# Four blocks of w_out instead of two in the slots of the projections' weights

## The chip, the cores and the metric

The kernel runs on one core of a Trainium2 chip. Its time is the device time of one execution in microseconds; before the change the median of three runs is 1167.86 us (1167.72 to 1168.35). Besides, one execution was recorded by the hardware profiler: it took 1168.21 us, of which 1166.4 lie between its first and its last instruction (the span). All rows below are from that execution.

The engines of a core work in parallel, each in its own order: TensorE (PE; its weight loads are listed as PEld) multiplies matrices into PSUM banks, VectorE (DVE) and ScalarE (ACT) work element by element, SyncE (SP) issues the transfers between HBM and the on-chip memory (SBUF), one after the other.

## The reference

The reference is one block of a hybrid transformer on x of 1024 positions by 1024 channels, in float32. An input projection `u = x @ w_in` feeds three branches: a gated causal convolution (256 channels), a chunked mLSTM (256 channels) and a differential attention with four heads (512 channels). Then:

```
h = concatenate([y_conv, y_ml, y_da]) @ w_out        # 1024 x 1024
x = layer_norm(ALPHA * x + h, ln1_g, ln1_b)
h = square(relu(x @ w_up)) @ w_down                  # 4096 hidden channels
x = layer_norm(ALPHA * x + h, ln2_g, ln2_b)
```

The change concerns the product with `w_out` and the residual `ALPHA * x`.

## The kernel before

**Precision.** Every float32 operand of a large product is split in two: ScalarE rounds it (`act.copy`, line 147, written `hi`, `th`, `yh`), VectorE subtracts the rounded value from the original (line 148, written `lo`, `tl`, `yl`). A product is the sum of three matmuls: hi x hi, lo x hi, hi x lo. A block of weights (128 x 1024) thus takes three slots while it is split, raw, hi and lo, and two after.

**Slots.** The SBUF buffers are 47 slots of 128 x 1056 words (`Slots`, line 54). Each ring is a queue of slot numbers: `alloc` takes the first, `free` appends at the end, so the order of allocations in the program decides which older buffer a new one lies in, and the new one's first writer waits for the last reader of the old. Ring X (slots 0 to 15) holds x, split; ring W (nine slots, 16 to 24) the weights of the input projections; ring T two slots for the projections' results; ring G the rest.

**Order.** A scheduler places the instructions of each engine when the program is built; a `lane` gives their priority: 1 (loads, splits, evacuations) goes before 2 (the mLSTM and the attention), 3 (the projections) and 6 (the output projection). The order is fixed in the program then, and each engine follows it and waits where it must.

**The place.** TensorE interleaves the attention of heads 0 to 2 with the input projections. The last of them (`proj_last`, line 193) goes through x in eight steps and frees two slots of X after each. Its two results lie in the two PSUM banks of `ps_mm` until ScalarE has written `th` and VectorE `tl`, half by half; these go to HBM (`qk<-th`, `qk<-tl`).

Behind it comes the output projection in two parts. Part one (`row1`, line 914) takes the first five blocks of `w_out`: 128 positions at a time (row 0 to row 7), two banks of 15 matmuls each, 240 in all; VectorE then adds ALPHA times the residual row, which was loaded from x (`acc<-in_x`, line 894). For each row five pieces of the branches' outputs are loaded (`yraw`) and split (`yh`, `yl`). Part one fills TensorE while the attention's heads 2 and 3 wait for ScalarE and VectorE. In the attention, `s` are scores, `pp` their exponentials, `t` the transposed ones, `wth` and `wtl` their halves, and `t<-wth,vh` and its like the product with the values. Part two (`row2`) takes blocks 5 to 7 (`wo2`), which lie in slots that part one frees, during the attention of head 3. Then follow the two large products with `w_up` and `w_down`.

The lines around the change:

```
839    early = [load_split(W, a["w_out"][kb], D) for kb in range(NEARLY)]
871                xa = (W if tb < NW - 2 * NEARLY else X).alloc(F32, "acc")
872                load(xa[:, :D], a["x"][tb])
917            early += [load_split(X, a["w_out"][kb], D) for kb in range(NEARLY, 5)]
918        row1(tb, [t for t in ((0, 1) if tb == 0 else (tb + 1,)) if t < TB])
919    for r, w in zip([W] * NEARLY + [X] * (5 - NEARLY), early):
920        r.free(*w)
921    X.give(W.take(2 * NEARLY))
```

With NEARLY = 2 blocks 0 and 1 go to W (their slots are those of earlier projections), blocks 2, 3 and 4 to slots that x leaves. Rows 0 to 4 of the residual (tb < 9 - 4) go to W, rows 5 to 7 to X.

Of the kernel before, what the change touches and what calls it, by code (L numbers as in the profile page):

```python
# [26 lines left out]
NSLOT = 47  # L27
NW = 9
NT = 2
NEARLY = 2  # L30
TCARGS = dict(schedule_with_timeline_sim=False)
EPS = 1e-5
ALPHA = 2.0 ** 0.25
# [64 lines left out]
def mixer_block(ctx: ExitStack, tc: tile.TileContext, a: dict, out: bass.AP):  # L98
# [18 lines left out]
    def load(out, in_):  # L117
        nc.sync.dma_start(out=out, in_=in_)
# [43 lines left out]
    def load_split(ring, src, n, ahead=True):  # L162
        with lane(1) if ahead else nullcontext():
            raw = ring.alloc(F32, "raw")
            load(raw[:, :n], src)
            h, l = ring.alloc(F32R, "hi"), ring.alloc(F32R, "lo")
            split(raw[:, :n], h[:, :n], l[:, :n])
            ring.free(raw)
        return h, l
# [483 lines left out]
    def proj_head(h):  # L653

        for j in range(2):
            th, tl = T.alloc(F32R, "th"), T.alloc(F32R, "tl")

            def take(half, cs, ps):
                if j == 0:
                    act.activation(th[:, cs], ps, AF.Copy, scale=0.125)  # L660
                    dve.scalar_tensor_tensor(out=tl[:, cs], in0=ps, scalar=0.125,
                                             in1=th[:, cs].bitcast(F32), op0=ALU.mult,
                                             op1=ALU.subtract)
                else:
                    split(ps, th[:, cs], tl[:, cs])

            (proj_last if 2 * h + j == 7 else proj_fm)(8 + 2 * h + j, take)
            with lane(1):
                move(qkdram[h][2 * j], th[:, :S])
                move(qkdram[h][2 * j + 1], tl[:, :S])  # L670
            T.free(th, tl)
# [166 lines left out]
    proj_head(3)  # L838
    early = [load_split(W, a["w_out"][kb], D) for kb in range(NEARLY)]
    qk_of, v_of = {}, {}  # L840
# [12 lines left out]
    def out_proj(kbs, first, wo, yring):  # L853
# [10 lines left out]
        def get_y(tb, ln, fetched=None):  # L864
            with ln(1):
# [4 lines left out]
                if first:  # L870
                    xa = (W if tb < NW - 2 * NEARLY else X).alloc(F32, "acc")
                    load(xa[:, :D], a["x"][tb])
# [42 lines left out]
    for tb in range(TB):  # L915
        if tb == 0:
            early += [load_split(X, a["w_out"][kb], D) for kb in range(NEARLY, 5)]
        row1(tb, [t for t in ((0, 1) if tb == 0 else (tb + 1,)) if t < TB])
    for r, w in zip([W] * NEARLY + [X] * (5 - NEARLY), early):
        r.free(*w)  # L920
    X.give(W.take(2 * NEARLY))
    X.give(G.take(6))
# [626 lines left out]
```

## Time and profile before

| | |
|---|---|
| median of three runs | 1167.86 us (1167.72 to 1168.35) |
| profiled execution, its span | 1168.21 us, 1166.4 us |
| TensorE busy | 1136.2 us, 97% of the span |
| VectorE, ScalarE busy | 830.8 us (71%), 577.5 us (50%) |
| TensorE's share of the chain that ended last | 85% |

TensorE is busy nearly all the time, and the chain of work that ended last runs mostly through it. So the time is TensorE's work, plus the stretches in which it waits, plus those in which its clock is granted at the lower of its two levels (1.2 instead of 2.4 GHz). A matmul's row shows its start and its length; the next one starts before its end, since they are pipelined, so the distance of starts is what one costs. In square brackets behind an instruction stands how long its engine was idle before it, and what ended that.

### The profile page before, as it was taken

Reading aid. Unit: us, or ns where it says so; the run is one execution under the profiler, and the core shown is the slowest. Engines: PE = TensorE matmul, PEld = TensorE weight load, DVE = VectorE, ACT = ScalarE, POOL = GpSimd, SP = SyncE. Lnnn points to the kernel's source line nnn. Section 1 sums busy time; section 2 is a strip of 40 time slices with the busy share of each in tenths; the row PEclk is TensorE's granted clock in tenths of the full one; section 3 lists DMA queues with packets and bytes.
Section 4 is the critical chain, followed back from the end, with each engine's and each line's share of the span. In section 5 each row is a group of like instructions: output and inputs, shape, how many; then the busy total and the mean of one; then the engine's idle time right before and its main releaser. Section 6 shows DMA issues by size and latency. Waiting matters only on the chain.

```text
span 1166.4 us, 14925 instructions
## 1 busy us (share of the span) xinstructions
PE 1136.2 (97%) x5630; PEld 930.8 (80%) x5630; DVE 830.8 (71%) x1243; ACT 577.5 (50%) x934; POOL 0.2 (0%) x4
## 2 busy tenths in 40 slices
PE   8999999999999999899999999999999999999996
PEld 6898778877897787677788888888888878888884
DVE  5999658875756547778986767655589677666686
ACT  6212383475665526596654444544545323334461
POOL 0000000000000000000000000000000000000000
PEclk9999999999999999999999999999999999999998
DMA  7202135444635663350466464534894644344321
GB/s 281 73 10 73 37 91 168 154 140 123 196 107 172 213 183 103 111 177 37 153 237 250 165 239 168 204 126 162 307 352 162 198 163 160 111 151 125 104 109 72
DMA packets 81640, 179.86 MB, mean 154 GB/s; under 512 B 7648, under 2 KB 29216, under 8 KB 81568
## 3 DMA queue, kind: packets, MB, share of 16 engines
q1 hardware_dynamic: 81568, 178.91, 45.1%
q8 instruction: 44, 0.72, 0.3%
q14 instruction: 28, 0.23, 0.1%
HBM read 120.12 MB, written 58.72 MB: 153 GB/s over the span
## 4 chain that ended last, share of the span: by engine, by line
PE 85%; DVE 7%; DMA 3%; ACT 3%; issue 2%; SPq 0%; DVEq 0%; ACTq 0%
PE f L944 32%; PE mm L112 26%; PE mm L944 17%; PE s L112 5%; PE t L112 3%; PE t L115 2%; DVE lo L148 1%; DMA kh<-qk 1%; ACT pp L738 1%; DVE acc L967 1%; DMA xraw<-in_xT 0%; DMA vh<-v 0%; DMA hraw<-h 0%; DVE nm L736 0%; DVE pp L744 0%
## 5 line engine op out<-in xcount | busy, mean ns | idle before, releaser
L944 PE MATMUL f<-hi 128*128 128x512 f32 x512 | 201.7, 394 | 1.4 <-DVE acc L1242 1.1
L944 PE MATMUL f<-lo,hi 128*128 128x512 f32 x512 | 201.5, 394 | 0.6 <-DVE lo L148 0.5
L944 PE MATMUL f<-hi,lo 128*128 128x512 f32 x512 | 201.5, 394 | 0.0
L944 PE MATMUL mm<-lo,hi 128*128 128x512 f32 x320 | 125.9, 394 | 0.3 <-DVE lo L148 0.3
L944 PE MATMUL mm<-hi 128*128 128x512 f32 x320 | 126.2, 394 | 0.0
L944 PE MATMUL mm<-hi,lo 128*128 128x512 f32 x320 | 126.1, 394 | 0.0
L944 PEld LDWEIGHTS f<-hi 128*128 128x128 f32 x512 | 96.5, 188 | 24.1 <-DVE acc L1242 1.5
L944 PEld LDWEIGHTS f<-lo,hi 128*128 128x128 f32 x512 | 96.3, 188 | 23.3 <-DVE lo L148 1.5
L944 PEld LDWEIGHTS f<-hi,lo 128*128 128x128 f32 x512 | 96.1, 188 | 22.1
L112 PE MATMUL mm<-xh,hi 128*128 128x512 f32 x240 | 95.8, 400 | 5.1 <-ACT xh L147 5.1
L147 ACT CAST hi<-hraw 128x1024 fp32r<-128x1024 f32 x56 | 58.2, 1048 | 84.9 <-DMA hraw<-h 83.4
L148 DVE TENSOR_TENSOR lo<-hraw,hi 128x1024 fp32r<-128x1024 f32 x56 | 68.2, 1223 | 44.6 <-ACT hi L147 42.4
L112 PE MATMUL mm<-xl,hi 128*128 128x512 f32 x240 | 96.1, 400 | 0.1
L112 PE MATMUL mm<-xh,lo 128*128 128x512 f32 x240 | 96.0, 400 | 0.0
L285 DVE SCALAR_TENSOR_TENSOR cacc<-ypad,pc,cacc 128x1024 f32<-128x1024 f32 x60 | 74.2, 1285 | 0.6
L112 PE MATMUL mm<-hi,xh 128*128 128x256 f32 (+1 forms) x256 | 74.1, 289 | 0.0
L112 PE MATMUL mm<-hi,xl 128*128 128x256 f32 (+1 forms) x256 | 73.2, 286 | 0.0
L112 PE MATMUL mm<-lo,xh 128*128 128x256 f32 (+1 forms) x256 | 73.1, 286 | 0.0
L944 PEld LDWEIGHTS mm<-lo,hi 128*128 128x128 f32 x320 | 60.2, 188 | 14.4 <-DVE lo L148 0.7
L944 PEld LDWEIGHTS mm<-hi 128*128 128x128 f32 x320 | 60.3, 188 | 13.8 <-DVE acc L967 0.3
L944 PEld LDWEIGHTS mm<-hi,lo 128*128 128x128 f32 x320 | 60.1, 188 | 13.8
L147 ACT CAST hi<-B 128x1024 fp32r<-128x1024 f32 x36 | 37.6, 1049 | 52.9 <-PE mm L944 23.9
(278 smaller groups left out, 2309.7 us busy)
## 6 DMA issues: line engine op xcount, KB each, us to landing
hraw<-h SPq DMA_DIRECT2D x56, 512.0 KB, 3.4
w<-in_w_up SPq DMA_DIRECT2D x32, 512.0 KB, 4.5
B<-in_w_down SPq DMA_DIRECT2D x32, 512.0 KB, 4.8
h<-hp SPq DMA_DIRECT2D x16, 512.0 KB
h<-hx SPq DMA_DIRECT2D x16, 512.0 KB, 3.1
h<-hq SPq DMA_DIRECT2D x16, 512.0 KB, 3.3
raw<-in_wfm SPq DMA_DIRECT2D x14, 512.0 KB, 3.5
qk<-th SPq DMA_DIRECT2D x8, 512.0 KB
```

The costliest lines, as they stand in the source:

```text
L112: return nc.tensor.matmul(out, lhsT=lhsT, rhs=rhs, start=start, stop=stop)
L115: nc.tensor.transpose(out, in_, ident[:k, :k])
L147: act.copy(hi, src)
L148: dve.tensor_tensor(out=lo, in0=src, in1=hi.bitcast(F32), op=ALU.subtract)
L285: dve.scalar_tensor_tensor(out=av, in0=yp[:, i:i + S], scalar=col(PC_DWW + 31 * c + i), in1=av, op0=ALU.mult, op1=ALU.add)
L738: act.activation(pp[m][:, 0:nk], s_[:, 0:nk], AF.Exp, bias=nm[:, m:m + 1], accum_out=sm[:, m:m + 1])
L944: return nc.tensor.matmul(out, lhsT=lhsT, rhs=rhs, start=start and not more, stop=stop and not more, skip_group_check=more)
L967: dve.tensor_tensor(out=out, in0=p, in1=q, op=ALU.add)
```

## The change

```diff
-NEARLY = 2
+NEARLY = 4
```

With NEARLY = 4 the same lines do this. Blocks 0 to 3 of `w_out` go to W, block 4 alone to X. Of the residual rows only row 0 lies in W (tb < 9 - 8), rows 1 to 7 in X. Following the queue of W: block 2 gets the slots 16, 17 and 18 for raw, hi and lo, which are raw, hi and lo of the last projection's own weights; block 3's raw goes to block 0's raw slot, its hi to block 1's, its lo to block 2's; row 0 of the residual goes to block 3's raw slot. After part one W hands eight slots to X instead of four. The number of slots in use, of transfers, splits and matmuls is the same.

The scheduler's order changes with it. On VectorE, between the end of the last projection and row 0 of part one, before (`lo_4076`, `lo_4082`, `lo_4088`: blocks 2, 3, 4; `tl_2762`: the last projection's two halves; `yl_4098`: row 0; `wtl_...`: attention; `acc_4101`: sum of row 0):

```order
L148 TENSOR_TENSOR lo_4076<-raw_4073,hi_4075 128x1024
L148 TENSOR_TENSOR lo_4082<-raw_4079,hi_4081 128x1024
L148 TENSOR_TENSOR lo_4088<-raw_4085,hi_4087 128x1024
L148 TENSOR_TENSOR tl_2762<-mm_2769,th_2761 128x512
L148 TENSOR_TENSOR tl_2762<-mm_2770,th_2761 128x512
L148 TENSOR_TENSOR yl_4098<-yraw_4091,yh_4097 128x640
L148 TENSOR_TENSOR wtl_3819<-t_3845,wth_3817 128x4x128
L148 TENSOR_TENSOR wtl_3820<-t_3852,wth_3818 128x128
L894 SCALAR_TENSOR_TENSOR acc_4101<-acc_4101,mm_4116 128x512
L148 TENSOR_TENSOR wtl_3819<-t_3880,wth_3817 128x4x128
L148 TENSOR_TENSOR yl_4110<-yraw_4103,yh_4109 128x640
L148 TENSOR_TENSOR wtl_3820<-t_3887,wth_3818 128x2x128
```

and now (`lo_4088`: block 4; `lo_2840`, `lo_2846`: blocks 2 and 3):

```order
L148 TENSOR_TENSOR lo_4088<-raw_4085,hi_4087 128x1024
L148 TENSOR_TENSOR yl_4098<-yraw_4091,yh_4097 128x640
L148 TENSOR_TENSOR tl_2762<-mm_2769,th_2761 128x512
L148 TENSOR_TENSOR lo_2840<-raw_2837,hi_2839 128x1024
L148 TENSOR_TENSOR tl_2762<-mm_2770,th_2761 128x512
L148 TENSOR_TENSOR lo_2846<-raw_2843,hi_2845 128x1024
L148 TENSOR_TENSOR yl_4110<-yraw_4103,yh_4109 128x640
L148 TENSOR_TENSOR wtl_3831<-t_3857,wth_3829 128x4x128
L148 TENSOR_TENSOR wtl_3832<-t_3864,wth_3830 128x128
L148 TENSOR_TENSOR wtl_3831<-t_3892,wth_3829 128x4x128
L894 SCALAR_TENSOR_TENSOR acc_4101<-acc_4101,mm_4116 128x512
L894 SCALAR_TENSOR_TENSOR acc_4101<-acc_4101,mm_4133 128x512
```

The two `tl` stood behind all three blocks; now the first stands behind block 4 and row 0's `yl`, the second behind block 2. Row 1's `yl` has moved up, and both sums of row 0 now stand together, ahead of the last `wtl`.

On TensorE, a little later, at the first score product after the attention's next product with the values, before (`t_3892`: product with the values; `mm_4133`: row 0, second bank; `s_3988`: scores):

```order
L112 MATMUL t_3892<-wth_3818,vh_3620 128x256
L112 MATMUL t_3892<-wtl_3820,vh_3620 128x256
L112 MATMUL t_3892<-wth_3818,vl_3621 128x256
L112 MATMUL t_3892<-wth_3818,vh_3620 128x128
L112 MATMUL t_3892<-wtl_3820,vh_3620 128x128
L112 MATMUL t_3892<-wth_3818,vl_3621 128x128
L112 MATMUL mm_4133<-hi_4075,yl_4098 128x512
L112 MATMUL s_3988<-kh_3526,q_3523 128x512
L112 MATMUL s_3988<-kl_3529,q_3523 128x512
```

and now (`t_3904`, `s_4000` the same two; `mm_4163`: row 1, first bank):

```order
L112 MATMUL t_3904<-wth_3830,vh_3632 128x256
L112 MATMUL mm_4163<-hi_2827,yh_4109 128x512
L112 MATMUL t_3904<-wtl_3832,vh_3632 128x256
L112 MATMUL t_3904<-wth_3830,vl_3633 128x256
L112 MATMUL t_3904<-wth_3830,vh_3632 128x128
L112 MATMUL t_3904<-wtl_3832,vh_3632 128x128
L112 MATMUL t_3904<-wth_3830,vl_3633 128x128
L112 MATMUL s_4000<-kh_3538,q_3535 128x512
L112 MATMUL s_4000<-kl_3541,q_3535 128x512
```

Ahead of the scores 24 matmuls of part one stood, now 31; the one that stood directly ahead of them is gone, and one of row 1 is put in between the products.

On TensorE, at the first score product of head 3 that reads the second half of its keys, before (`mm_4351`: row 5, first bank; `s_4529`: these scores):

```order
L112 MATMUL mm_4351<-hi_4075,yh_4297 128x512
L112 MATMUL mm_4351<-lo_4076,yh_4297 128x512
L112 MATMUL mm_4351<-hi_4075,yl_4298 128x512
L112 MATMUL mm_4351<-hi_4081,yh_4297 128x512
L112 MATMUL s_4529<-kh_3937,q_3934 128x128
L112 MATMUL s_4547<-kh_3928,q_3925 128x256
```

and now (`mm_4368`: row 5, second bank):

```order
L112 MATMUL mm_4351<-hi_4087,yl_4298 128x512
L112 MATMUL mm_4368<-hi_2827,yh_4297 128x512
L112 MATMUL mm_4368<-lo_2828,yh_4297 128x512
L112 MATMUL mm_4368<-hi_2827,yl_4298 128x512
L112 MATMUL mm_4368<-hi_2833,yh_4297 128x512
L112 MATMUL s_4529<-kh_3949,q_3946 128x128
L112 MATMUL s_4547<-kh_3940,q_3937 128x256
```

Ten matmuls of row 5 stood ahead of the scores, now nineteen.

## Rows read from the trace of the kernel before

**Rows 1.** Stretches: per engine busy us (instructions), granted clock, DMA share, GB/s.

```profile
388.00:391.40 3.40, 3.39 (x8) 2.72 (x9) 1.88 (x3) 0.72 (x2) 0.00 (x0) 0.52 1.00 330
...
510.00:540.00 30.00, 28.43 (x146) 23.14 (x144) 22.67 (x52) 25.70 (x40) 0.00 (x0) 1.00 0.29 110
540.00:570.00 30.00, 28.83 (x122) 22.15 (x123) 29.96 (x33) 20.19 (x25) 0.00 (x0) 1.00 0.10 36
600.00:630.00 30.00, 30.00 (x131) 24.31 (x130) 22.57 (x27) 14.67 (x19) 0.00 (x0) 1.00 0.55 196
```

**Rows 2.** TensorE waits, 385 to 550 us: us in total, times, longest.

```profile
PE mm L112 <- DVE tl L148: 2.5, 1, 2.5
PE mm L112 <- DVE lo L148: 1.7, 2, 1.4
PE mm L112 <- DVE yl L148: 1.6, 1, 1.6
PE s L112 <- DMA kh<-qk: 1.0, 1, 1.0
```

**Rows 3.** Timeline of TensorE, end of the last projection: start, length, instruction.

```profile
384.43 0.39 PE L112 MATMUL mm<-xh,lo 128*128 128x512 f32 x1
...
385.13 0.40 PE L112 MATMUL mm<-xh,lo 128*128 128x512 f32 x1
388.01 0.77 PE L112 MATMUL mm<-hi,yh 128*128 128x512 f32 x1 [2.48 <-DVE tl L148]
```

**Rows 4.** Timeline of ScalarE, the same place.

```profile
382.47 1.05 ACT L147 CAST hi<-raw 128x1024 fp32r<-128x1024 f32 x1 [4.76 <-DMA raw<-in_w_out]
...
385.91 1.07 ACT L147 CAST th<-mm 128x512 fp32r<-128x512 f32 x2
386.86 0.74 ACT L147 CAST yh<-yraw 128x640 fp32r<-128x640 f32 x1
```

**Rows 5.** Timeline of VectorE, the same place.

```profile
383.55 3.71 DVE L148 TENSOR_TENSOR lo<-raw,hi 128x1024 fp32r<-128x1024 f32 x3 [5.32 <-ACT hi L147]
387.18 1.28 DVE L148 TENSOR_TENSOR tl<-mm,th 128x512 fp32r<-128x512 f32 x2
```

**Rows 6.** Timeline of SyncE's DMA issues, the same place.

```profile
377.24 3.05 SPq L118 DMA_DIRECT2D raw<-in_w_out  x3
381.14 4.30 SPq L118 DMA_DIRECT2D yraw<-ydram  x8
...
388.48 0.32 SPq L121 DMA_DIRECT2D qk<-tl  x1
```

**Rows 7.** DMA issues, 386 to 392 us: count, KB each, us to landing.

```profile
qk<-tl SPq DMA_DIRECT2D x1, 512.0 KB, 2.8
```

**Rows 8.** Timeline of ScalarE near 397 us.

```profile
397.25 1.01 ACT L738 ACTIVATE pp<-s,nm 128x896 f32<-128x896 f32 x1 [1.83 <-PE t L112]
```

**Rows 9.** Timeline of TensorE near 397 us.

```profile
395.58 0.31 PE L112 MATMUL t<-wth,vh 128*128 128x256 f32 x1
...
397.57 0.27 PE L112 MATMUL t<-wth,vl 128*128 128x128 f32 x1
...
398.40 0.50 PE L112 MATMUL s<-kh,q 128*128 128x512 f32 x1 [0.27 <-ACT pp L738]
```

**Rows 10.** Timeline of TensorE near 439 us.

```profile
439.09 0.49 PE L112 MATMUL s<-kh,q 128*128 128x128 f32 x2 [1.05 <-DMA kh<-qk]
```

**Rows 11.** Timeline of SyncE's DMA issues near 430 us.

```profile
428.84 1.80 SPq L118 DMA_DIRECT2D acc<-in_x  x2
430.68 1.09 SPq L121 DMA_DIRECT2D kh<-qk  x2
```

**Rows 12.** Timeline of TensorE near 470 us.

```profile
468.84 0.83 PE L115 MATMUL t<-cst,pp 128*128 128x128 f32 x6
...
470.90 0.34 PE L112 MATMUL t<-wth,vh 128*128 128x256 f32 x1
```

**Rows 13.** Timeline of SyncE's DMA issues near 476 us.

```profile
476.00 0.33 SPq L118 DMA_DIRECT2D raw<-in_w_out  x1
```

## The prediction

> **What bounds the kernel now.** I read the table of stretches first [rows 1]. From 600 us on TensorE works 30.00 of every 30 us, and so it goes on to the end: what is gained or lost before 550 us is carried to the last instruction. The reader should then look at the slice 388.0 to 391.4: 8 matmuls and a granted clock of 0.52, mostly the lower of the two levels. The list of TensorE's waits between 385 and 550 us [rows 2] has one entry above all others, 2.5 us behind a VectorE subtraction for `tl`. In TensorE's own timeline [rows 3] it is seen in place: the last projection's last matmul starts at 385.13 and ends at 385.53, the first of row 0 of the output projection starts at 388.01. Before the gap matmuls stand (385.13 - 384.43) / 3 = 0.23 us apart, in the slow slice 3.40 / 8 = 0.43. So this place costs 2.48 us of idleness and 8 x (0.43 - 0.23) = 1.6 us of slow clock.
>
> Why it waits: row 0 needs a PSUM bank that the last projection's result holds until it is cast (`th`) and its rest subtracted (`tl`). ScalarE casts three blocks of w_out from 382.47, and `th` only at 385.91 [rows 4]; VectorE spends 3.71 us from 383.55 on the three blocks' low halves, and `tl` starts at 387.18 [rows 5]. The three blocks are this late because their buffers are slots of x, which the last projection frees as it runs: SyncE issues the loads at 377.24 [rows 6].
>
> **The change part by part.** It adds and removes no instruction; five blocks are loaded and split in either kernel, eight residual rows loaded. It moves blocks 2 and 3 from x's slots to W's, and residual rows 1 to 4 the other way. What was to land in W must still wait for W: block 2's halves go into the slots of the last projection's own weights, so its cast cannot start before that projection's last matmuls; block 3's low half goes into block 2's raw slot. Only block 3's high half and block 4 are ready ahead. So the work between the projections is not removed, but VectorE's order changes: `tl` of the first half now stands ahead of the low halves of blocks 2 and 3.
>
> Term A, the gap. The first half's last matmul starts at 384.43 and lasts 0.39 [rows 3]: 384.82. A `th` cast is 1.07 / 2 = 0.54 [rows 4], a `tl` 1.28 / 2 = 0.64 [rows 5], and in the trace TensorE starts 0.19 after the first `tl` ends (387.18 + 0.64 = 387.82 to 388.01). A hand-over from ScalarE to VectorE takes little (a cast over at 382.47 + 1.05 = 383.52, the subtraction at 383.55); with 0.1 for each of the two that is 386.4, so the gap is 0.9 and 1.6 us are saved. Both casts ahead of `th` must be over: block 4's load is the only one issued at 377.24, landing in at most 382.47 - 377.24 = 5.2 us, cast in 1.05 to 383.5; five loads of `yraw` follow at 4.30 / 8 = 0.54 each [rows 6], so the last leaves at 380.3; with the 2.8 us of a larger transfer [rows 7] it lands at 383.1 and `yh` (0.74 [rows 4]) ends at 384.3, just early enough; with 5.2 us it lands at 385.5 and 1.4 of the 1.6 are lost. Bounds 0.2 to 1.8; I take 1.6, since the queue is empty there but for these loads. What is late next: block 2's low half. Its cast follows `th` at 385.4 and ends at 386.5, its subtraction (3.71 / 3 = 1.24) at 387.8; TensorE has 7 matmuls ahead of it in its order and comes to it at 386.4 + 7 x 0.23 = 388.0. The second bank is wanted after 10 matmuls (388.7) and free at 387.8 + 0.64 = 388.4. Block 3's low half ends at 388.4 + 1.24 = 389.7 and is wanted after 14 (389.7). None of the three stops TensorE by more than 0.1.
>
> Term B, the clock. The idle stretches behind `lo` (1.4) and `yl` (1.6) [rows 2] left the clock at 1.00 (510 to 540 us, [rows 1]), so one of 0.9 should too: 1.6 us saved, bounds 0 and 1.6. The Trainium skill (TensorE: Matmul & The Clock Gate, Part 1: The HAM clock gate) calls the number of slow matmuls "run-variable", because the monitor runs free of the kernel; by that rule no gap is sure to leave the clock alone, and the sum would lack this term. The trace has one slow stretch, behind its longest gap, and none behind the shorter ones, so I keep the term and make the rule a rival.
>
> Term C, the residual of row 0. Its slot is now block 3's raw one, so its load can be issued only at 389.7, behind `qk<-tl` at 388.48 [rows 6]. In VectorE's order the sum of row 0 stands ahead of a `wtl` subtraction that TensorE wants for the attention's second product, after 31 matmuls of the output projection, 6 transposes (0.83 at most [rows 12]) and 13 products of 128 or 256 columns, (397.57 - 395.58) / 17 = 0.12 each [rows 9]: 386.4 + 7.2 + 0.8 + 1.5 = 395.9. I take two sums and the `wtl` like a `tl`, 0.64 each, 1.9 together. A landing 2.8 us after issue [rows 7] is in time (392.5 + 1.9 = 394.4). At 5.2 it is not (396.8, a wait of 0.9). Then comes the next score product: it waits for an exponential of 1.01 us that starts as the second product ends [rows 8, 9]. Before, one matmul covered part of that (0.27 idle); now none does, 0.3 more. Bounds -1.2 and 0; I take -0.4, near the short landing, the nearest row in time and queue.
>
> Term D, the wait for `kh`. In the trace TensorE stands 1.05 us at 439.09 behind a transfer [rows 10] whose issue at 430.68 follows two residual rows at 428.84 [rows 11], released by TensorE itself. That release comes about 2.8 us earlier (A, B, C), and in the new order nine more matmuls of the output projection (9 x 0.23 = 2.1 us) stand ahead of the same score product. TensorE gets there some 0.7 us earlier than now, the transfer 2.8: the wait goes, 1.05 saved, bounds 0 and 1.05.
>
> Term E, where the first part of the output projection runs out. Now six of its matmuls cover the transposed scores' split: transposes at 468.84, product at 470.90 [rows 12]. In the new order one is left there: of 2.06 us some 0.8 stay filled, a new wait of 1.2. In exchange block 7's load, at 476.00 [rows 13] because its slot is freed by the very last of those matmuls, comes that much earlier against the work that wants it, and the 1.4 us behind `lo` [rows 2] shrink to perhaps 0.4. Sum -0.2, bounds -1.2 and +1.7.
>
> After 550 us nothing moves but the names of buffers. VectorE is busy 29.96 of 30 us from 540 to 570 [rows 1]; its work there follows the same rows, so I let it shift with them.
>
> Sum: 1.6 + 1.6 - 0.4 + 1.05 - 0.2 = 3.65 us. From the profiled execution, 1168.21 us (span 1166.4), that gives 1164.6; the median of three runs, 1167.86, lies 0.35 lower, so I predict 1164.2 us.
>
> **The rivals.**
> R1, the clock still falls. Without B the gain is 2.05: 1165.8 us. For it: the one fall came at this very place. Against it: the stretches of 1.4 and 1.6 us without one.
> R2, spent early and waited for later. A and B come, but the attention's own chain keeps its pace; C costs 1.0 of its 1.2, D is not gained, E costs its 1.2: 3.2 - 2.2 = 1.0, 1166.9 us. For it: in the new order the filling matmuls stand further forward at every place I compared (7, then 9, then 5 of them), and VectorE is full from 540. Against it: the named waits apart, no entry in the list of 385 to 550 exceeds 1.0 us [rows 2], so most places have slack.
> R3, slower: the residual row, now late. The transfer for `kh` took from its last issue at 431.2 to 439.05, 7.8 us [rows 10, 11]. If row 0's load does so, it lands at 397.5, the `wtl` is done at 399.4, TensorE stands 3.5 us and the clock falls again, 1.6. Against the 3.2 of A and B, with nothing from D and E, that is 1.9 lost: 1169.8 us. It decides from a landing about 4 us after issue; each further microsecond costs one, and beyond some 2.5 us of idleness the slow clock comes on top. Against it: few transfers are in flight at 390 us.
> That the change does nothing because block 2 must wait anyway is not a case of its own: VectorE's order settles it.
>
> **How the numbers follow.** The forecast 0.52 (its own range 1162.6 to 1165.6), R1 0.11, R2 0.26, R3 0.11. A measurement of this kernel tells about 0.2%, 2.3 us, from no change, so faster means below 1165.5: nearly all of the forecast and a part of R1, and a little of R2, 0.56. Within 0.2%: the rest of R1 and most of R2, 0.33. Slower: R3, 0.11. The range 1162.0 to 1168.4 leaves out some 0.08 below (E at its best) and 0.11 above.
>
> **What would show it.** A: TensorE's gap at the end of the last projection about 0.9 us, first `tl` ahead of two `lo`. B: no stretch near 0.5 of the clock after it. C: the sum of row 0 on VectorE behind a transfer, and no wait of TensorE over 1 us near 396. D: no `kh` in the list of waits. E: a wait behind `wtl` near 467, a shorter one behind `lo`. A sum of TensorE's waits between 385 and 550 that is not about 2 us smaller would make the prediction wrong, and so would a gap of 2 us or more at its old place.

## The result, and the profile after

The changed kernel takes 1162.06 us (median of five, 1161.27 to 1163.77), 0.9947 of the kernel before (95% interval 0.9937 to 0.9958): 5.8 us faster, where 3.65 were predicted. Measured twice more on other chips it is 0.9943 [0.9931, 0.9954] and 0.9957 [0.9944, 0.9969]. The profiled execution took 1163.77 us, span 1162.0.

The stretches after, with the columns of [rows 1]:

```profile
388.00:391.40 3.40, 3.40 (x15) 2.74 (x16) 3.23 (x4) 1.30 (x4) 0.00 (x0) 1.00 0.69 272
472.40:476.00 3.60, 3.52 (x19) 3.52 (x19) 3.60 (x7) 2.85 (x5) 0.00 (x0) 0.59 0.53 165
510.00:540.00 30.00, 29.99 (x161) 24.84 (x160) 24.63 (x52) 25.78 (x39) 0.00 (x0) 1.00 0.22 89
```

Right behind the last projection 15 matmuls run at the full clock, where 8 ran at 0.52. But a stretch with a clock of 0.59 now stands at 472.4. From 510 to 540 TensorE is busy 29.99 us instead of 28.43.

TensorE's waits between 385 and 550 us, to be held against [rows 2]:

```profile
PE t L112 <- DVE wtl L148: 1.9, 1, 1.9
PE s L112 <- DMA kh<-qk: 1.0, 1, 1.0
PE mm L112 <- DVE tl L148: 0.7, 1, 0.7
PE f L944 <- DVE lo L148: 0.5, 1, 0.5
PE t L112 <- ACT sqs L147: 0.3, 1, 0.3
PE mm L112 <- DVE acc L897: 0.3, 1, 0.3
PE s L112 <- ACT pp L738: 0.3, 1, 0.3
PE mm L112 <- DVE lo L148: 0.3, 1, 0.3
```

`tl` 2.5 is 0.7, `lo` 1.7 is 0.3, `yl` 1.6 is gone; `kh` stays; `wtl` 1.9 is new. (`sqs` are the rounded squares for a head's norm, the `acc` of line 897 is a sum of part two; further below, `sm` are the sums of the softmax and `mvf` the statistics of the layer norm.) The projection's end in TensorE's timeline, beside [rows 3]:

```profile
386.88 0.40 PE L112 MATMUL mm<-xh,lo 128*128 128x512 f32 x1
387.98 0.50 PE L112 MATMUL mm<-hi,yh 128*128 128x512 f32 x1 [0.70 <-DVE tl L148]
```

On ScalarE, beside [rows 4], `th` follows the last matmul of its half at once, with only one block (382.72) and row 0's `yh` in front:

```profile
382.72 1.05 ACT L147 CAST hi<-raw 128x1024 fp32r<-128x1024 f32 x1 [3.26 <-DMA raw<-in_w_out]
385.12 0.73 ACT L147 CAST yh<-yraw 128x640 fp32r<-128x640 f32 x1 [1.34 <-DMA yraw<-ydram]
386.61 0.59 ACT L147 CAST th<-mm 128x512 fp32r<-128x512 f32 x1 [0.77 <-PE mm L112]
```

On VectorE, beside [rows 5], `tl` follows it:

```profile
385.88 0.83 DVE L148 TENSOR_TENSOR yl<-yraw,yh 128x640 fp32r<-128x640 f32 x1 [0.85 <-DMA yraw<-ydram]
387.23 0.69 DVE L148 TENSOR_TENSOR tl<-mm,th 128x512 fp32r<-128x512 f32 x1 [0.53 <-ACT th L147]
388.17 1.23 DVE L148 TENSOR_TENSOR lo<-raw,hi 128x1024 fp32r<-128x1024 f32 x1 [0.25 <-ACT hi L147]
```

SyncE, beside [rows 6], issues one block, not three, ahead of the rows of y, and row 0's residual at 391.16:

```profile
378.99 0.33 SPq L118 DMA_DIRECT2D raw<-in_w_out  x1
379.66 5.46 SPq L118 DMA_DIRECT2D yraw<-ydram  x10
...
391.16 0.33 SPq L118 DMA_DIRECT2D acc<-in_x  x1
```

The new wait near 472 us: TensorE's last matmul of part one at 470.11, the product at 472.48.

```profile
469.54 0.82 PE L115 MATMUL t<-cst,pp 128*128 128x128 f32 x6
470.11 0.47 PE L112 MATMUL mm<-hi,yl 128*128 128x512 f32 x1
472.48 0.38 PE L112 MATMUL t<-wth,vh 128*128 128x256 f32 x1 [1.89 <-DVE wtl L148]
```

On VectorE `wtl` could start when its first cast is over, near 470.6 (ScalarE runs the two from 470.18 for 0.86 us); block 6's low half and row 7's sum stand ahead of it:

```profile
470.01 1.22 DVE L148 TENSOR_TENSOR lo<-raw,hi 128x1024 fp32r<-128x1024 f32 x1
471.14 0.68 DVE L894 SCALAR_TENSOR_TENSOR acc<-acc,mm 128x512 f32<-128x512 f32 x1
471.74 0.69 DVE L148 TENSOR_TENSOR wtl<-t,wth 128x512 fp32r<-128x512 f32 x1
```

Blocks 6 and 7 are loaded earlier than before (462.30 and, [rows 13], 476.00):

```profile
455.85 0.33 SPq L118 DMA_DIRECT2D raw<-in_w_out  x1
```
```profile
471.60 0.38 SPq L118 DMA_DIRECT2D raw<-in_w_out  x1
```

### The profile page after: what moved, and what is told of

Read it like the earlier page. It is cut to its first block, busy times and chain, and to the rows that moved or that the text cites. A ratio compares the mean times of both kernels' runs of the same rounds, so it can differ in the third digit from the quotient of the medians.

```text
span 1162.0 us, 14933 instructions
## 1 busy us (share of the span) xinstructions
PE 1135.4 (98%) x5630; PEld 931.4 (80%) x5630; DVE 832.1 (72%) x1243; ACT 578.5 (50%) x934; POOL 0.2 (0%) x4
## 4 chain that ended last, share of the span: by engine, by line
PE 86%; DVE 7%; DMA 3%; ACT 2%; issue 1%; SPq 0%; DVEq 0%; ACTq 0%
PE f L944 32%; PE mm L112 26%; PE mm L944 17%; PE s L112 5%; PE t L112 4%; PE t L115 2%; DVE lo L148 1%; DMA kh<-qk 1%; DMA xraw<-in_xT 1%; DVE nm L736 1%; DVE acc L967 1%; ACT pp L738 0%; ACT hi L147 0%; DMA vh<-v 0%; DVE pp L744 0%
```

## The experiments

All are compared with the kernel before on the same chip; the table gives in each kernel's profile the wait in front of row 0 (us), the idle stretches over 0.2 us added up from TensorE's timeline from 5 us behind the projection's end to 560 (the last three of them, 1.1 us in all, are the same in every kernel and lie between 538 and 556), the start of part one's last sum on VectorE, and the number of half-clock stretches before the kernel's end.

| kernel | row 0 | 392 to 560 | last sum | half clock | ratio [95%] |
|---|---|---|---|---|---|
| before | 2.48 | 8.0 | 476.2 | 1 | 1 |
| changed, three profiles | 0.70, 0.70, 1.00 | 5.2, 5.2, 5.5 | 471.1, 469.9, 470.8 | 1, 0, 0 | 0.9947, 0.9943, 0.9957 |
| e1 order, first try | 3.45 | 6.9 | 482.3 | 1 | 1.0028 [1.0019, 1.0037] |
| e12 order alone | 1.30 | 5.4 | 470.4 | 0 | 0.9938 [0.9924, 0.9951] |
| e2 three blocks | 2.03 | 5.1 | 471.9 | 1 | 0.9955 [0.9942, 0.9967] |
| e3 block 6 behind | 0.70 | 7.0 | 472.7 | 0 | 0.9962 [0.9949, 0.9974] |
| e5 row 7 behind too | 0.70 | 7.4 | 471.3 | 0 | 0.9966 [0.9954, 0.9978] |
| e4, e10 free slots first | 0.70, 0.80 | 5.0, 4.8 | 467.7, 468.3 | 0, 0 | 0.9937 [0.9924, 0.9949], 0.9943 [0.9930, 0.9955] |
| e6 before, free first | 2.44 | 5.4 | 476.8 | 1, twice as long | 0.9975 [0.9962, 0.9988] |
| e7 three, free first | 2.27 | 4.4 | 476.7 | 1 | 0.9961 [0.9949, 0.9973] |
| e9 free first, tuned | 0.70 | 3.3 | 467.4 | 0 | 0.9924 [0.9910, 0.9938] |

**e1: the order without the slots.** In the kernel before, block 4's split stays where it was and those of blocks 2 and 3 are queued behind the projection's first half (comment added):

```diff
+            get_y1(0, lane)
+            with lane(1), behind(*thtl[-2]):
+                for raw, hi, lo in late:      # blocks 2 and 3
+                    split(raw[:, :D], hi[:, :D], lo[:, :D])
```

> The kernel before, with its slots as they are (two blocks of w_out in W, three in x's), but the casts and subtractions of blocks 2 and 3 queued behind those of the last projection's first half and behind row 0's, as they stand in the changed kernel. Theory (terms A and B come from the order on ScalarE and VectorE alone): the wait of 2.48 us falls to about 0.8, no half-clock stretch behind it, so 1.7 + 1.6 = 3.3 us less before 392 us; what follows 470 us stays within 1 us of the kernel before: 1164.6 us. Rival (the changed kernel's gain is not made there but behind 470 us, where blocks 6 and 7 are loaded earlier, and what is saved at the projection's end is waited for later): 1167.5 us or more, with the saved time back as longer waits before 520 us.

Slower, 1171.43 us: neither theory. On ScalarE:

```profile
388.41 1.04 ACT L147 CAST hi<-raw 128x1024 fp32r<-128x1024 f32 x1 [7.62 <-PE mm L112]
389.36 1.07 ACT L147 CAST th<-mm 128x512 fp32r<-128x512 f32 x2
390.31 1.06 ACT L147 CAST hi<-raw 128x1024 fp32r<-128x1024 f32 x1
391.26 0.73 ACT L147 CAST yh<-yraw 128x640 fp32r<-128x640 f32 x1
```

Block 4's cast, now first in the queue, starts only at 388.41; its load is the third of three issued from 380.32 to 383.37. Everything queued behind it is late, row 0's `yh` too. The trace names TensorE as what the cast waited for, but the load alone would have held it nearly as long: in the kernel before, the third load left at 379.97 and its block was cast when it had landed, at 384.95, 4.98 us later; here the third left at 383.05, 5.36 before the cast. So this was not the order of the changed kernel, where the block in front is the only one loaded there; and `yh` stands behind block 2's cast, not ahead of `th`: the edit queues blocks 2 and 3 behind the projection's first half alone, not behind row 0's too, as was meant. Part one ends 6 us later than before. What the kernel lost beyond this wait is not settled by its one profile: six of the eleven executions have a mean clock of 0.993, the profiled one 0.996.

**e12: the order alone, mended.** Block 4 is loaded and cast first, then come the projection's halves and row 0's y, then blocks 2 and 3:

```diff
+            last = load_split(X, a["w_out"][4], D)
+            for kb in (2, 3):
...
+            with lane(1), behind(*thtl[-2], *y_split[0]):
```

> The kernel before, slots and loads where they were, with the order alone mended better than in the first experiment: block 4 is loaded and cast first of the three, then both halves of the last projection, then row 0's y, and only then blocks 2 and 3. Theory of the prediction (VectorE's order makes the wait of 2.48 us): the first matmul of row 0 waits 0.9, no half-clock stretch in most executions, 2 to 3 us less than the kernel before: 1165.5 us. Rival (row 0's y and blocks 2 and 3 are late because three loads of half a megabyte are issued ahead of y near 377 us, and only the freed slots take two of them away): the wait in front of row 0 stays at 1.5 or more, or comes again within a few matmuls behind lo, with the same sum; 1167 us or more, and half-clock stretches as before.

1161.72 us, with no half clock in any of five executions (mean clock 0.997 or 0.998): the whole gain, with two blocks in W as before; of the three in x's slots block 4 is loaded first, and so takes the slots that block 2 had. TensorE's waits, same view as above:

```profile
PE mm L112 <- DVE acc L901: 1.7, 2, 1.4
PE t L115 <- DVE pp L746: 1.3, 2, 1.1
PE mm L112 <- ACT yh L147: 1.3, 1, 1.3
PE s L112 <- DMA kh<-qk: 0.7, 2, 0.4
```

No `yl`, no `lo` of a block; row 0 waits 1.3 for `yh`. More went than the theory's 2 to 3 us: behind 392 us 5.4 instead of 8.0. Here too part one ends earlier (470.4 instead of 476.2), and block 7's load left at 470.21, 5.8 us earlier than before [rows 13]. The rival falls: the three loads ahead of y cost at most the 0.6 between 1.30 and 0.70.

**e2: three blocks.** `NEARLY = 3`.

> Three blocks in W instead of two or four. The order on VectorE has two low halves ahead of the first half of the last projection's rest instead of three (before) or one (changed), and at the end of the first part of the output projection five matmuls beside the transposes instead of six (before) or one (changed), with block 6's low half behind the transposed scores' rest. Theory (the changed kernel's new wait of 1.9 us near 472 us, and the clock's fall behind it, come from block 6's low half standing in front and from the missing filling): a gap of 1.3 at the projection's end, no half-clock stretch anywhere before the end of the span, no wait behind wtl; the wait behind block 7's low half about 1.0. Against the changed kernel +0.6 -1.9 -1.6 +0.7 = 2.2 us less: 1159.9 us. Rival (the waits that vanished in the changed kernel behind 480 us, 2.7 us in all, hang on blocks 6 and 7 being loaded 4 to 6 us earlier, which three blocks do not bring): 1162.5 us. Rival two (one fall of the clock happens wherever the longest gap is): one half-clock stretch behind the gap of 1.3, 1161.5 to 1164 us.

1163.14 us. As expected there is no wait near 472; but row 0 waited 2.0, not 1.3, with a half clock behind it (by the mean clock in four executions of five), and new waits came near 493 and 497. The theory's 1159.9 falls; the time and the place of the stretch are those of rival two, and rival one's time is as near:

```profile
PE mm L112 <- ACT yh L147: 2.0, 1, 2.0
PE t L112 <- DVE wtl L148: 1.4, 1, 1.4
PE mm L112 <- DVE acc L897: 1.4, 1, 1.4
```

**e3 and e5: the wait near 472.** In the changed kernel, block 6's low half queued behind `wtl` (e3); then also the sums for w_up and row 7's second sum (e5; shown in part, comments added). In both, the first four rows of part two come later in the program, with rows 4 and 5:

```diff
+            with lane(5), behind(last_wtl[0]):
+                dve.tensor_tensor(out=wo2[1][1][:, :D], in0=raw6[:, :D], ...
...
+                w_sums(0)                     # e5
+                w_split(0, "w1")              # e5
...
+            with lane(1), behind(last_wtl[0]):   # e5: row 7's second sum
...
```

> The changed kernel with the subtraction for block 6's low half queued on VectorE behind the transposed scores' rest (wtl) that TensorE waits for near 472 us; the rows of the second part are traced later in the program for it. Theory: the subtraction of 1.22 us in front makes most of the wait of 1.9; without it the wait is 0.7, and the clock does not fall: 1.2 + 1.6 = 2.8 us less than the changed kernel, 1159.3 us. Rival one: the wait is that of the cast and of row 7's sum, 1.5 or more stay and the clock falls as before: 1161.7 us. Rival two: block 6's low half, now late, is waited for at the start of the second part: of the 2.8 only the clock's 1.6 is kept, or nothing: 1160.5 to 1162 us.

1163.75 us. Nearest to rival one, for another reason: the wait grew to 2.69, since the scheduler put a sum for w_up in the empty place, which waits for its load:

```profile
472.08 0.69 DVE L969 TENSOR_TENSOR wx<-w 128x512 f32<-128x512 f32 x1 [1.23 <-DMA w<-in_w_up]
472.69 0.68 DVE L896 SCALAR_TENSOR_TENSOR acc<-acc,mm 128x512 f32<-128x512 f32 x1
473.29 1.02 DVE L148 TENSOR_TENSOR wtl<-t,wth 128x512 fp32r<-128x512 f32 x2
```

And behind this longer wait the clock did not fall in the profiled execution (three of the five have a mean clock of 0.995):

```profile
474.00:477.40 3.40, 3.33 (x22) 2.86 (x23) 3.40 (x6) 2.43 (x7) 0.00 (x0) 1.00 0.35 144
```

> The changed kernel with everything on VectorE that can wait queued behind the transposed scores' rest (wtl) that TensorE wants near 472 us: block 6's low half, the four sums for w_up that took its place in the run before this one, and row 7's second sum. Theory: wtl then follows its cast at once; the wait of 1.9 us falls to 0.8, and the clock does not fall behind so short a gap: 1.1 + 1.6 = 2.7 us less than the changed kernel, 1159.4 us. Rival one (the gap's length does not decide on the clock): 1.1 less, but a half-clock stretch in most executions, 1161.0 us. Rival two (the delayed work is waited for behind it: row 7's bank by the second part's first row, block 6's low half by its fourth matmul): the 1.1 come back as waits between 474 and 486 us: 1160.5 to 1162 us.

The wait itself fell to 0.95, as the theory says, but the time was 1165.19 us: rival two, in size beyond it, and by the mean clock (0.995 or 0.996) four executions of five have a half clock. The waits moved behind it; the first three of the list:

```profile
PE t L112 <- DVE wtl L148: 1.9, 2, 1.0
PE t L115 <- DVE mvf L810: 1.3, 1, 1.3
PE mm L112 <- DVE yl L148: 1.3, 1, 1.3
```

**e4 and e6: blocks 5 to 7 loaded early.** The six slots that the finished heads leave go to the front of the queue, in the changed kernel (e4) and in the kernel before (e6); the three loads are then issued from 437 (e4) or 439 us (e6) on.

```diff
+    X.q.extendleft(reversed(G.take(6)))
     X.give(W.take(2 * NEARLY))
-    X.give(G.take(6))
```

> The changed kernel, with the six slots that the finished heads leave put at the front of the queue of free slots instead of at its end, so that blocks 5 and 6 (and the raw of block 7, one turn earlier) are loaded some 10 us sooner. Theory (what vanished in the changed kernel behind 480 us came from blocks 6 and 7 being loaded earlier): the waits behind lo stay away, block 6's low half is done long before 470 us, so the wait of 1.9 behind wtl shrinks to 0.7 and the clock does not fall: 1159 us. Rival (the three low halves, 3.7 us of VectorE, now stand in front of the rests that the attention wants at 445 to 465 us): new waits of 1 to 3 us there, 1162 to 1164 us.

1160.98 us. The wait near 472 and the half clock are gone; waits of 1.25 (`sqs`) and 1.22 (`yl`) came, at 495 and 511 us, so the sum stays at 5.0, and the time lies between the theory's and the rival's.

> The kernel before, with the six slots that the finished heads leave put at the front of the queue of free slots, so that blocks 6 and 7 are loaded some 10 us sooner; nothing else is changed, and up to 440 us nothing moves. Theory (what vanished in the changed kernel behind 480 us hangs on blocks 6 and 7 being loaded sooner): of the waits behind lo 1.4 and 0.35, sm 0.62, acc 0.55 and yl 1.55 some 3 us go: 1165.2 us. Rival (it hangs on the matmuls of the first part standing further forward, which here they do not): the waits behind lo go, 1.7 us, but the one behind yl stays and the time hidden is waited for elsewhere: 1167 to 1168 us.

1167.10 us over seven executions. The waits fell from 8.0 to 5.4, as the theory says, `lo` and `yl` among them, although the first part stands no further forward; but a new one of 3.1 came, as the rival says, and the time is the rival's:

```profile
PE mm L112 <- ACT yh L147: 3.1, 1, 3.1
PE mm L112 <- DVE tl L148: 2.4, 1, 2.4
```

Behind the wait of 3.1 (at 479.35, for a row of part two) stands a half clock twice as long as any other. The three executions with a mean clock of 0.995 or more took 1164.4 to 1164.7, near the theory's 1165.2, the four below it, the profiled one among them, 1167.1 to 1169.3.

**e7: three blocks and the free slots first.** 

> Three blocks in W, and the free slots first. With three blocks alone TensorE waited 2.03 us at the projection's end with a half-clock stretch behind it in most executions, and 1.44 behind wtl and 1.38 behind a sum near 491 and 497 us. Theory (sooner blocks take the pressure off VectorE behind 480 us, as they did with four blocks, where no wait over 1.25 us was left): 2 us of these two waits go: 1161.1 us. Rival (with the three low halves now between 440 and 465 us, new waits of the same sum come up there or later): 1162.5 to 1163.5 us.

1164.97 us. The two waits went (4.4 in all), but row 0 waits 2.27, by the mean clock the half clock is there in every execution, and part one ends at 476.7: the time is above the rival's too, and by the ratio there is no gain over e2.

**e8, e11: the changed kernel again.**

> The changed kernel once more, beside the runs that are compared with it. 1162.1 us. If the half-clock stretch near 472 us belongs to this kernel, every execution has one (mean clock 0.995 or 0.996, where an execution without one has 0.997); if it is chance, some executions have none and are about 1.6 us shorter.

> The changed kernel a third time, as the partner of the two before it: 1162.2 us; half-clock stretches in some executions and not in others, with under 1 us between the two kinds.

1162.27 and 1163.81 us. It is chance: by the mean clock four of these ten executions have no half clock, and both profiled ones show the same wait behind `wtl` and no fall of the clock behind it (below, e8). But they are not 1.6 us shorter: in e8 1162.11 to 1162.51 without it, 1162.27 and 1163.75 with it; in e11 1162.51 without, 1163.29 to 1163.99 with it.

```profile
471.23 0.39 PE L112 MATMUL t<-wth,vh 128*128 128x256 f32 x1 [1.89 <-DVE wtl L148]
```
```profile
471.20:474.70 3.50, 2.84 (x20) 2.40 (x20) 3.40 (x6) 2.80 (x5) 0.00 (x0) 1.00 0.56 179
```

**e10, e9: a version that beats both.** e10 is e4 again. e9 adds two moves:

```diff
+    get_y(6, here, last_y[0])
     x1_half(0, lambda: (bank(), bank()))
...
+    with behind(*last_sqs):
+        w_split(0, "x")
```

> The changed kernel with the free slots first, once more, beside the changed kernel itself on the same chip. Theory (no wait over 1.3 us and no half-clock stretch): 1161.0 us, and at least 1 us under the changed kernel beside it. Rival (the clock's stretch costs next to nothing over a whole execution, and the sums of the waits are equal): within 0.5 us of it.

> The changed kernel with the free slots first (as in an earlier run, 1160.98 us), and two moves against the waits that were left there: row 6's y is split ahead of the first half of the norm's transposes (the wait of 1.22 us behind yl), and the cast of w_up's sum is queued behind the last cast of the head's squares (the wait of 1.25 us behind sqs). Theory (each of the two waits is one instruction of another kind in front, with nothing else due there): both go, 2.2 us: 1158.8 us. Rival (as with row 7's sum, what is put back is wanted soon after, and the sum of TensorE's waits between 390 and 545 us stays near 5): 1160 to 1161 us.

e10: 1161.74 us beside 1163.81 of the changed kernel, 2.1 less, as the theory says, but the intervals overlap. e9: 1159.18 us, as the theory says, 0.9924 against 0.9957, intervals apart: 9 us under the kernel before. The wait behind `yl` went, that behind `sqs` fell to 0.8, and nothing took their place:

```profile
PE t L112 <- ACT sqs L147: 0.8, 1, 0.8
PE mm L112 <- ACT yh L147: 0.8, 1, 0.8
PE mm L112 <- DVE tl L148: 0.7, 1, 0.7
```

## Why the prediction was right in its place and wrong in its size

**What bounds the kernel, and the place:** right. The wait that was read out of [rows 2, 3] is the one that went, and what was gained there stayed in the time.

**Term A (1.6): right.** 2.48 fell to 0.70 in the first profile (that of the section on the result), 1.78 us less, and to 0.70 and 1.00 in the repeats (e8, e11). The cause named, the order on ScalarE and VectorE, holds: e12 gets 1.30 and the time with the order alone (its edit moves casts and subtractions together and does not part the two engines). e1 shows the condition: what stands ahead of `th` has to be ready.

**Term B (1.6): right at its place, not sure to be kept.** The slow slice behind the projection is gone. In the first profile another stands behind the 1.89 of `wtl`: there the product's 18 matmuls take 475.95 - 472.48 = 3.47 us, in e8 473.39 - 471.23 = 2.16. These 1.3 are not what it cost, for the next score product follows without a wait in the first profile and waits for `pp` in e8:

```profile
476.71 0.39 PE L112 MATMUL s<-kh,q 128*128 128x512 f32 x1
```
```profile
474.93 0.50 PE L112 MATMUL s<-kh,q 128*128 128x512 f32 x1 [0.86 <-ACT pp L738]
```

From the product's start to the scores pass 4.23 us there, 3.70 in e8 and 3.62 in e11: 0.5 to 0.6 lost. Over executions the mean clock allows an estimate of how often a stretch comes: profiles without one show 0.997, those with one 0.995 or 0.996. Of 45 executions of the kernel before three show 0.997, 34 one of these two, eight less (0.993 or 0.994, taken as two stretches); of 15 of the changed kernel four none and eleven one. That is (34 + 16) / 45 = 1.1 stretches against 0.7. At 1.6 each that would be 0.6 us, and at 0.5 far less; what B is worth over executions is not shown. The reading behind the term holds, for that trace has no other half-clock stretch before the kernel's end, but the row cited for it shows half of it: of the two waits only that behind `yl` lies between 510 and 540 us, that behind `lo` is at 480.51. The rule that was weighed, that the slow matmuls are "run-variable" (the Trainium skill, TensorE: Matmul & The Clock Gate, Part 1: The HAM clock gate), agrees with the runs: one kernel, one wait of 1.9, clock 0.59 in one execution and 1.00 in two.

**Term C (-0.4): too dear.** The next score product waits 0.32 against 0.27 [rows 9]. Row 0's load left at 391.16, but its sum starts right behind a `wtl`, with no idle time of VectorE ahead of it. R3 did not come.

**Term D (1.05): not a term.** The wait behind `kh` was 0.98 in the first profile. In the repeats it is missing, as forecast, in e12 0.30, in e3 1.43, in e4, e5 and e9 missing; but it is missing in e6 too, whose kernel is the one before up to 440 us. It is a transfer that lands sooner or later from one execution to the next; one execution cannot tell its price. The wait behind `vh` near 366 (0.27 before, 1.06 after, none in e8, 0.94 in e1) and the first matmul (5.06 before, 5.00 after, 6.88 in e1) are of the same kind.

**Term E (-0.2, bounds -1.2 to +1.7): the step that failed.** "Sum -0.2" looked at two waits, the new one behind `wtl` and the shrinking one behind `lo`. Both came as said in kind: 1.9 for 1.2 and 0.3 for 0.4. But the list [rows 2] held more in that stretch, and nothing was worked out for it. In TensorE's timeline between 455 and 520 the waits before were 0.54 and 0.27 (`pp`), 1.40 and 0.34 (`lo`), 0.62 (`sm`), 0.33 and 0.55 (`acc`), 1.55 (`yl`): 5.60. After: 0.35 (`sqs`), 1.89 (`wtl`), 0.31 (`lo`), 0.32 (`acc`): 2.87 in the first profile, where the slow clock hides the wait for `pp`; with that wait 3.76 in e8 and 4.14 in e11. So E measured +1.8 and +1.5 where the clock stayed, at its upper bound, and +2.7 where it fell, before the cost of the slow clock: 1.7 to 2.9 us more than the -0.2.

The row that gave it away was used for one wait alone: block 7's load comes 476.00 - 471.60 = 4.4 us earlier, block 6's 6.5. In e6, whose one edit is to load these blocks sooner, the sum falls from 8.0 to 5.4, although a new wait of 3.1 comes. The largest of the waits before, `yl`, hangs on the order. Before, on VectorE and TensorE:

```profile
517.41 0.56 DVE L148 TENSOR_TENSOR yl<-yraw,yh 128x384 fp32r<-128x384 f32 x1
```
```profile
518.02 0.50 PE L112 MATMUL mm<-hi,yl 128*128 128x512 f32 x1 [1.55 <-DVE yl L148]
```

and after, on VectorE:

```profile
513.57 0.55 DVE L148 TENSOR_TENSOR yl<-yraw,yh 128x384 fp32r<-128x384 f32 x1
```

Before, row 6's `yh` was cast at 512.75, but its `yl` stood behind four results of the norm's transposes on VectorE; after, it stands behind three, and 30 of these transposes instead of 20 stand directly ahead of row 6 on TensorE (510.20 to 513.64), so it is in time. The order that the scheduler writes down moves with the slots and loads; what of E is due to the loads themselves and what to the order that came with them was not separated.

**The sum.** From the end of the last projection to a matmul that every kernel has (`mm<-lo,hi`, behind a wait of 0.3 for `lo`, at 551.92 before) TensorE took 551.92 - 385.53 = 166.4 us before, 548.44 - 387.28 = 161.2 in the first profile after, 159.5 in e8 and 160.2 in e11: 5.2, 6.9 and 6.2 us less. In the two with the clock up, A to D came to 4.4 and 4.1, against 3.85 forecast; with E that is 6.2 and 5.5. In the first A, C and D gave 1.8, the two slow stretches cancel, and E gave 2.7: 4.5. The 0.7 that are missing each time lie in no idle stretch over 0.2 us and in no half clock, and were not taken apart. What stands ahead of this stretch is chance: the projection ended 1.7 to 1.9 us later in all three, and 2.0 later in e6, where nothing is changed up to there. What lies behind it took 1.0 less in the first profile, 0.6 of that a shorter wait behind 930 us: the two profiles differ by 5.2 - 1.8 + 1.0 = 4.4. R2 named what happened (`wtl` took its price) but not what was given back. R1 came in one profile of three, at another place.

## What to carry to other kernels

When a stall ahead of a long stretch of filling work goes, follow the slots which that work frees: their next loads move with it, and every wait that hangs on them has to be priced, not only the one that is read first. Before buffers are moved, try the order alone, that of the loads with it: here it was worth as much as the slots (e12). A wait behind a transfer in one profile is a sample. A wait of TensorE that is taken away by queueing other work behind what it waits for can come back (e5) or stay away (e9), as that work is soon wanted or not. And a stretch at the half clock costs only what TensorE would not have waited anyway: here 0.5 to 0.6 us of 1.3.

## What was not expected of the hardware

In the profiled executions the length of a wait did not decide on the clock: it fell behind 1.89 us in one execution of the changed kernel and not behind 1.89 and 1.88 in two others, not behind 2.44 in e6 and not behind 2.69 in e3, so the "some 2.5 us" of R3 does not hold. Behind 3.14 in e6 the half clock lasted twice as long (from 479.4 to 486.2 us the mean is 0.59).
